# Gated linear attention by levels: multiplying queries and keys in place by exponentials of block totals

## The chip, the cores and the metric

The kernel runs on one core of a Trainium2 chip. A core has a matrix engine (TensorE, PE in the profile, with PEld for the loading of its weights), a vector engine (VectorE, DVE), a scalar engine (ScalarE, ACT), a general engine (GpSimd, POOL) and queues that issue transfers (SyncE, SP, among them). Each engine runs its own list of instructions in order and waits on semaphores for the others. The metric is the device time of one execution in microseconds (us); lower is better.

## The reference, cut to what matters

One decoder layer: a token mixer of two parallel branches, gated linear attention (GLA) and latent attention (MLA), and then a squared-ReLU MLP, each followed by a layer norm. 512 tokens, width 1024, all in float32. The branch that the change touches is GLA, with 4 heads of 128 key channels and 256 value channels:

```python
h = layer_norm(x, ln_in_g, ln_in_b)
q_g, k_g, v_g, r_g, a_lr, q_lat, kv_lat, gate_logits = split(h @ w_in)
log_a = log_sigmoid(a_lr @ w_gla_a2 + b_gla_a2) / 16          # per token and key channel, <= 0
# per head: S_t = diag(exp(log_a_t)) S_{t-1} + k_t^T v_t ;  o_t = q_t S_t, that is
# o_i = sum over j <= i of  ( sum_d q[i,d] k[j,d] exp(b[i,d] - b[j,d]) ) v_j ,   b = running sum of log_a
y_gla = (rms_norm(o) * silu(r_g)) @ w_o_gla
y_mla = softmax attention over q_lat, kv_lat ... @ w_o_mla
g_gla, g_mla = split(sigmoid(gate_logits + b_gate))
out = (g_gla * y_gla + g_mla * y_mla) @ w_out
```

## The kernel before

**Numbers.** Float32 accuracy is had by splitting each operand into a high part and a rest in a narrower format: a product costs three matmuls, high by high, high by rest and rest by high. A helper (`gemm_fm`, L231 to L233 in the profile, and `gemm_tm`, L264 to L266) runs these over 8 slices of the contraction, with four accumulators of 512 columns in PSUM for one section of 512 output columns. Weights come by DMA to `wraw`, ACT writes the high part `whi` (L180), DVE the rest `wlo` (L181).

**Sections and lanes.** The main line is a row of such sections: latents, q, k, then v (value, `proj_v`), r (output gate of GLA, `proj_r`), v, r, then four sections of the branch gates g0 to g3 with the rope part of the MLA queries between them, and so on. After each slice of a section, `tick` advances background generators: `t_lv`, which runs `gla_levels` for heads 0 to 3, and `t_out`, which runs `gla_out`, multiplies the scores by v, normalises and transposes (L735 to L774). A section can only begin in an accumulator when the section before it has been read out of it: for an r section by ACT (`th`, L600) and then DVE (`rg`, L603); for a gate section by ACT (`gt`, L958).

**Levels.** `gla_levels` builds the decayed scores of a head by doubling blocks: s = 1, 2, 4, ... 256. At level s every block of 2s tokens is cut into a left and a right half, and the scores between right queries and left keys need the decay from the key's place to the end of the left half and from the start of the right half to the query. The kernel keeps these exponents in a tile `rp` (row 0 for keys, row 1 for queries, filled by a copy at L623 and a memset at L624). Per level:

- ACT: `E` = exp(rp / 16), 512 columns, with left keys and right queries interleaved (L651);
- DVE: `M` = E times the matching columns of `qk`, written packed; two instructions of 256 columns up to s = 64 (L658), one of 512 above (L654);
- DVE: `advance` adds the block totals into `rp` for the next level (L634);
- PE: two 128x128 matmuls of packed M (L692; s = 128 at L695; for s = 256 transposes at L699);
- DVE: the scores are put into `SD` under a mask (L667), one level later.

For the diagonal, `products` multiplies q by k on POOL (`pr`, L614), ACT copies the high part (L616), POOL subtracts the rest (`qkp`, L617), and PE sums over channels (L682). `products` of the next head is called at level 16.

**What sets the order.** The Python code calls sections and generators in turn; the framework then orders the instructions of each engine by priorities and by its own estimates of durations, and places the waits. Tiles come from pools with a fixed number of buffers.

Of the kernel before, what the change touches and what calls it, by code (L numbers as in the profile page):

```python
# [10 lines left out]
F32 = mybir.dt.float32  # L11
# [8 lines left out]
P = 128  # L20
T = 512
# [31 lines left out]
def tile_hybrid_block(ctx: ExitStack, tc: tile.TileContext, I, out, dbg=None):  # L53
# [234 lines left out]
    for hp in range(2):  # L288
        PL["v", hp] = plan("w_in", C_V + hp * T, T)
        PL["r", hp] = plan("w_in", C_R + hp * T, T)  # L290
    def plan_qr(g):
        PL["qr", g] = plan("w_q_b", NOPE, 4 * ROPE, heads=(HQ, 4 * g, 4), per=4)

    for br in range(2):
        for mb in range(2):
            PL["g", br, mb] = plan("w_in", C_G + br * D + mb * T, T)
        plan_qr(br)

    def plan_pair(pr):
        PL["qn", pr] = plan("w_q_b", 0, 2 * P, heads=(HQ, 2 * pr, 2))  # L300
# [308 lines left out]

    QKP = [None] * GH  # L610

    def products(h, qk):
        pr = B([P, T], F32, "pr")
        gtt(pr, qk[:, 0, :], qk[:, 1, :], op=ALU.mult)  # L614
        QKP[h] = [B([P, T], F32R, "qkp") for _ in range(2)]
        act(QKP[h][0], pr, AF.Copy)  # L616
        gtt(QKP[h][1], pr, f(QKP[h][0]), op=ALU.subtract)  # L617

    def gla_levels(h):
        qk = QK[h]  # L620
        QK[h] = None
        rp = A([P, 2, T], F32, "rp")
        nc.vector.tensor_copy(rp[:, 1, :], GL[h])  # L623
        nc.gpsimd.memset(rp[:, 0, :], 0.0)  # L624
        SD = B([P, NT, P], F32, "SD")
        s128 = kq = None

        def advance(s):
            v = rp[:, 0, :]

            def view(off, side, step):
                return bass.AP(tensor=v.tensor, offset=v.offset + off, ap=[v.ap[0], [side, 2], [2 * s, T // (2 * s)], [step, s]])
            new = view(0, T + s, 1)
            vtt(new, new, view(T + 2 * s - 1, -s, 0), op=ALU.add)  # L634

        def half_lr(t2, s, i):
            v = t2[:, 0, :]
            return bass.AP(tensor=v.tensor, offset=v.offset + 2 * i * P,
                           ap=[v.ap[0], [2 * s, P // s], [T + s, 2], [1, s]])

        def packed(M, s, i):
            v = M[:, i, 0, :]
            return bass.AP(tensor=v.tensor, offset=v.offset,
                           ap=[v.ap[0], [2 * s, P // s], [s + (-2 * P if i else 2 * P), 2], [1, s]])

        def taken(v, s, step):
            return bass.AP(tensor=v.tensor, offset=v.offset + s, ap=[v.ap[0], [step, 2], [2 * s, P // s], [1, s]])

        def vec(s):
            E = B([P, T], F32, "E")  # L650
            act(pairs(E, s), lr(rp, s), AF.Exp, scale=1.0 / 16.0)  # L651
            if s > 64:
                M = B([P, T], F32, "M")
                vtt(pairs(M, s), pairs(E, s), lr(qk, s), op=ALU.mult)  # L654
            else:
                M = B([P, 2, 2, P], F32, "M")
                for i in range(2):
                    vtt(packed(M, s, i), pairs(E[:, 2 * i * P:2 * (i + 1) * P], s), half_lr(qk, s, i), op=ALU.mult)  # L658
# [24 lines left out]
        prev = None  # L683
        while s < T:
            if s == 2:
                vtt(SD, diag.rearrange("p (t i) -> p t i", i=P), ident[:, None, :].to_broadcast([P, NT, P]), op=ALU.mult)
            if s == 16 and h + 1 < GH:
                products(h + 1, QK[h + 1])
            p = PX()
            if s <= 64:  # L690
                for u in range(2):
                    mm(p[:, u * P:(u + 1) * P], M[:, 0, u, :], M[:, 1, u, :], start=True, stop=True)  # L692
            elif s == 128:
                for i in range(2):
                    mm(p[:, i * P:(i + 1) * P], M[:, 2 * i * P:(2 * i + 1) * P],  # L695
                       M[:, (2 * i + 1) * P:(2 * i + 2) * P], start=True, stop=True)
            else:
                for j in range(2):
                    nc.tensor.transpose(p[:, j * P:(j + 1) * P], M[:, j * P:(j + 1) * P], ident)  # L699
                kq = A([P, 2, 2, 256], F32R, "kq")  # L700
                split(M[:, 256:], kq[:, 1, 0], kq[:, 1, 1])
# [11 lines left out]
        act(sd[:, 0, :2], SD[:, :2], AF.Copy)  # L713
        gtt(sd[:, 1, :2], SD[:, :2], f(sd[:, 0, :2]), op=ALU.subtract)
        take(*prev)
        yield
        pt = p[:, :2 * P].rearrange("p (u i) -> p u i", i=P)
        split(pt, sd[:, 0, 2:], sd[:, 1, 2:])
        SS[h] = (sd, s128, kq)
        if h != 2:  # L720
            yield
# [218 lines left out]
            step(t_lv)  # L940

    WID[0] = 3
    proj_v(0)
    proj_r(0)
    finish(t_lat2)
    proj_v(1)
    proj_r(1)
    t_gla = [t_lv, t_out]


    gt = [None] * NK
    for br in range(2):
        for mb in range(2):
            def ev_g(a, ps):
                m = mb * 4 + a
                if gt[m] is None:
                    gt[m] = A([P, 2, T], F32, "gt")
                act(gt[m][:, br, :], ps, AF.Tanh, scale=0.5, bias=hbg[:, br * NK + m:br * NK + m + 1])  # L958
            gemm_fm(PL["g", br, mb], hT, T, ev_g)
        mla_qr(br)  # L960
    hT = None


# [361 lines left out]
```

## Time and profile before

| what | value |
|---|---|
| runs | 887.48, 888.38 and 892.6 us, median 888.38 |
| the profiled execution | 887.85 us |
| its span, first to last instruction | 885.9 us (1.95 us lie outside it) |
| PE busy | 863.7 us |
| DVE busy | 584.4 us |
| ACT busy | 438.9 us |
| POOL busy | 134.1 us |
| the levels on the time axis | first L692 matmul at 104.8 us, last at 253.0 us |

How to read it: "busy" is the time in which an engine had an instruction under way. Idle time of an engine that nobody waits for costs nothing, so what matters is when PE, the busiest, stood still, and what it then waited for. The granted clock (PEclk) is the share of the full TensorE clock; at 0.5 a matmul takes twice as long. In a timeline row the columns are start, duration, engine, line, operation, result<-operands, sizes, count, and in brackets idle time ahead of it and what ended it. Where a row has a count of more than one, its duration is from the first start to the last end.

### The profile page before, as it was taken

How to read it: one execution, taken by the hardware profiler on the slowest of the kernel's cores; microseconds unless marked ns; L12 is line 12 of the kernel's file. 1: busy time of each engine (PE TensorE's matmuls, PEld its weight loads, DVE VectorE, ACT ScalarE, POOL GpSimd, SP SyncE). 2: the span in 40 equal slices, each digit the busy share in tenths (PEclk: the TensorE clock that was granted, in tenths of full speed). 3: DMA queues.
4: the chain of work that ended last, by engine and by line, in shares of the span. 5: the costliest groups of instructions: out<-in, count | busy, mean ns of one | idle time of the engine just before them, and what ended most of it. 6: DMA issues, size and time to landing. Idle time of an engine off the chain costs nothing.

```text
span 885.9 us, 11470 instructions
## 1 busy us (share of the span) xinstructions
PE 863.7 (97%) x4336; PEld 735.9 (83%) x4336; DVE 584.4 (66%) x989; ACT 438.9 (50%) x737; POOL 134.1 (15%) x159
## 2 busy tenths in 40 slices
PE   5999999999999999999999999999999999999995
PEld 5988888887888888888888888988888888888884
DVE  7834894867665234557866797886557646754687
ACT  5546553634444334435654414565457546735661
POOL 2203320111002010000000013004400520242022
PEclk9999999999999999999999999999999999999998
DMA  7413223221323223111307628006941990398075
GB/s 235 145 48 95 72 72 95 72 72 48 90 72 88 74 84 101 54 43 54 116 25 264 190 71 285 1 0 164 293 114 29 260 253 28 71 305 195 1 189 96
DMA packets 63415, 101.13 MB, mean 114 GB/s; under 512 B 7777, under 2 KB 31764, under 8 KB 63360
## 3 DMA queue, kind: packets, MB, share of 16 engines
q1 hardware_dynamic: 48400, 64.04, 23.5%
q0 software_dynamic: 13040, 32.71, 15.5%
q10 hardware_dynamic: 1920, 3.66, 1.2%
q8 instruction: 34, 0.56, 0.3%
q14 instruction: 21, 0.17, 0.1%
HBM read 82.56 MB, written 3.67 MB: 97 GB/s over the span
## 4 chain that ended last, share of the span: by engine, by line
PE 95%; DVE 2%; ACT 1%; DMA 1%; issue 0%; POOL 0%; POOLq 0%; SPq 0%; DVEq 0%; ACTq 0%
PE mm L231 16%; PE mm L232 16%; PE mm L233 16%; PE mm L266 6%; PE mm L264 6%; PE mm L265 6%; PE px L1170 3%; PE px L1172 3%; PE px L1171 3%; PE mm L1170 2%; PE mm L1172 2%; PE mm L1171 2%; PE px L692 1%; PE px L868 1%; PE px L266 1%; PE px L265 1%
## 5 line engine op out<-in xcount | busy, mean ns | idle before, releaser
L181 DVE TENSOR_TENSOR wlo<-wraw,whi 128x1024 fp32r<-128x1024 f32 (+2 forms) x102 | 117.5, 1152 | 137.1 <-ACT whi L180 130.9
L231 PE MATMUL mm<-h,whi 128*128 128x512 f32 x416 | 163.3, 393 | 1.1 <-DVE rg L603 1.1
L232 PE MATMUL mm<-h,whi 128*128 128x512 f32 x416 | 163.0, 392 | 0.0
L233 PE MATMUL mm<-h,wlo 128*128 128x512 f32 x416 | 156.1, 392 | 0.0
L180 ACT ACTIVATE whi<-wraw 128x1024 fp32r<-128x1024 f32 (+2 forms) x102 | 99.9, 979 | 109.6 <-PE mm L232 66.3
L231 PEld LDWEIGHTS mm<-h,whi 128*128 128x128 f32 x416 | 78.6, 189 | 16.9 <-DVE rg L603 1.3
L232 PEld LDWEIGHTS mm<-h,whi 128*128 128x128 f32 x416 | 78.6, 189 | 16.0
L233 PEld LDWEIGHTS mm<-h,wlo 128*128 128x128 f32 x416 | 78.4, 189 | 16.1
L1198 POOL DMA_DIRECT2D res<-ev x54 | 47.5, 985 | 238.0 <-ACT ev L1196 190.7
L265 PE MATMUL mm<-wlo,h 128*128 128x512 f32 x128 | 50.5, 395 | 0.0
L266 PE MATMUL mm<-whi,h 128*128 128x512 f32 x128 | 50.3, 395 | 0.0
L264 PE MATMUL mm<-whi,h 128*128 128x512 f32 x128 | 49.2, 398 | 0.0
L1252 ACT ACTIVATE relu<-mm 128x512 f32<-128x512 f32 x32 | 18.8, 596 | 57.0 <-PE mm L233 57.0
L651 ACT ACTIVATE E<-rp 128x512 f32<-128x512 f32 x36 | 23.9, 665 | 28.3 <-DVE rp L634 27.4
L658 DVE TENSOR_TENSOR M<-E,qk 128x256 f32<-128x256 f32 x56 | 26.7, 501 | 15.4 <-ACT E L651 15.3
L355 POOL TENSOR_TENSOR mv<-mv,mhalf 128x1 f32<-128x1 f32 x4 | 4.1, 1036 | 208.9 <-DVE mv L354 208.9
L180 ACT ACTIVATE xh<-wraw 128x1024 fp32r<-128x1024 f32 (+1 forms) x20 | 19.0, 959 | 26.2 <-PE mm L266 15.0
L181 DVE TENSOR_TENSOR wlo<-wq,whi 128x1024 fp32r<-128x1024 f32 x15 | 18.4, 1224 | 20.3 <-ACT whi L180 20.3
L266 PEld LDWEIGHTS mm<-whi,h 128*128 128x128 f32 x128 | 24.1, 188 | 4.8
L265 PEld LDWEIGHTS mm<-wlo,h 128*128 128x128 f32 x128 | 24.1, 188 | 4.2
L264 PEld LDWEIGHTS mm<-whi,h 128*128 128x128 f32 x128 | 24.0, 188 | 4.1
L1196 ACT ACTIVATE ev<-mm 128x512 f32<-128x512 f32 x20 | 11.9, 600 | 29.6 <-DMA res<-ev 23.7
(400 smaller groups left out, 2223.6 us busy)
## 6 DMA issues: line engine op xcount, KB each, us to landing
wraw<-in_w_in_dram SPq DMA_DIRECT2D x40, 512.0 KB, 3.7
wraw<-in_w_ff_dram SPq DMA_DIRECT2D x32, 512.0 KB, 8.4
wq<-in_w_ff_dram POOLq DMA_DIRECT2D x32, 512.0 KB, 9.8
res<-ev POOLq DMA_DIRECT2D x54, 256.0 KB, 8.7
wraw<-in_w_o_gla_dram SPq DMA_DIRECT2D x8, 512.0 KB, 3.8
wraw<-in_w_o_mla_dram SPq DMA_DIRECT2D x8, 512.0 KB, 3.4
wraw<-in_w_out_dram SPq DMA_DIRECT2D x8, 512.0 KB, 4.3
wraw<-in_w_in_dram SPq DMA_DIRECT2D x8, 360.0 KB, 4.2
```

Of the source, the lines that this page charges most:

```text
L180: st["ins"] = act(hi[:, :nk, :n], raw[:, :nk, :n], AF.Copy)
L181: vtt(lo[:, :nk, :n], raw[:, :nk, :n], f(hi[:, :nk, :n]), op=ALU.subtract)
L231: mm(o, hi[:, c], xh, start=first, stop=False)
L232: mm(o, hi[:, c], xl, start=False, stop=False)
L233: mm(o, lo[:, c], xh, start=False, stop=last)
L264: mm(o, xh, hi[:, :n], start=opens, stop=False, skip_group_check=share)
L265: mm(o, xh, lo[:, :n], start=False, stop=False, skip_group_check=share)
L266: mm(o, xl, hi[:, :n], start=False, stop=last, skip_group_check=share)
L1170: mm(o, xh[:, c], hi[:, pp, cols], start=opens, stop=False, skip_group_check=True)
L1171: mm(o, xh[:, c], lo[:, pp, cols], start=False, stop=False, skip_group_check=True)
L1172: mm(o, xl[:, c], hi[:, pp, cols], start=False, stop=hf == 1 and pp == 1, skip_group_check=True)
L1198: nc.gpsimd.dma_start(res[tt + t][:, j * T:(j + 1) * T], e, accum_op=ALU.add)
```

## The change

The exponents are no longer kept and exponentiated level by level. `totals` (new) builds, on POOL, the sums of log_a over blocks of 2, 4, ... 128 tokens by seven pairwise additions (256, 128, ... 4 columns) into a tile `tot`; ACT takes the exponential of the log decays themselves in place (512 columns) and of all totals (508 columns). Queries are multiplied once by exp of their own decay (DVE). From then on, `grow(s)` multiplies, in place, the queries of right halves and the keys of left halves by the exponential of the total of the other half (DVE, 512 columns, in the place of `advance`). Since `qk` then holds what the level needs, packing is a copy: two ACT copies of 256 columns for each level up to 64 (`pack`); levels 128 and 256 read `qk` directly. `rp`, its copy and its memset, `E`, and the multiplications into `M` are gone. `totals` of the next head is called where `products` is, at level 16. A second edit changes the order of the gate sections: g0, g2, rope, g1, g3, rope in the place of g0, g1, rope, g2, g3, rope; the weight plan and the calls both follow one table.

```diff
+    ORDER = (("v", 0), ("r", 0), ("v", 1), ("r", 1), ("g", 0), ("g", 2), ("qr", 0), ("g", 1), ("g", 3), ("qr", 1))
...
+    def totals(h):
+        t = TOT[h] = B([P, T], F32, "tot")
+        src, o, n = GL[h], 0, T // 2
+        while n >= 4:
+            a = src.rearrange("p (n two) -> p n two", two=2)
+            src = t[:, o:o + n]
+            gtt(src, a[:, :, 0], a[:, :, 1], op=ALU.add)
+            o += n
+            n //= 2
+        act(GL[h], GL[h], AF.Exp, scale=1.0 / 16.0)
+        act(t[:, :o], t[:, :o], AF.Exp, scale=1.0 / 16.0)
...
     def gla_levels(h):
         qk = QK[h]
         QK[h] = None
-        rp = A([P, 2, T], F32, "rp")
-        nc.vector.tensor_copy(rp[:, 1, :], GL[h])
-        nc.gpsimd.memset(rp[:, 0, :], 0.0)
         SD = B([P, NT, P], F32, "SD")
...
-        def advance(s):
...
-            new = view(0, T + s, 1)
-            vtt(new, new, view(T + 2 * s - 1, -s, 0), op=ALU.add)
+        def grow(s):
+            new = view(qk[:, 0, :], 0, T + s, 2 * s, 1, s)
+            tot, o = (GL[h], 0) if s == 1 else (TOT[h], T - 2 * T // s)
+            vtt(new, new, view(tot, o + 1, -1, 2, 0, s), op=ALU.mult)
...
-        def vec(s):
-            E = B([P, T], F32, "E")
-            act(pairs(E, s), lr(rp, s), AF.Exp, scale=1.0 / 16.0)
-            if s > 64:
-                M = B([P, T], F32, "M")
-                vtt(pairs(M, s), pairs(E, s), lr(qk, s), op=ALU.mult)
-            else:
-                M = B([P, 2, 2, P], F32, "M")
-                for i in range(2):
-                    vtt(packed(M, s, i), pairs(E[:, 2 * i * P:2 * (i + 1) * P], s), half_lr(qk, s, i), op=ALU.mult)
-            if s < 256:
-                advance(s)
+        def pack(s):
+            M = B([P, 2, 2, P], F32, "M")
+            for i in range(2):
+                act(packed(M, s, i), half_lr(qk, s, i), AF.Copy)
             return M
...
         if h == 0:
+            totals(0)
             products(0, qk)
+        vtt(qk[:, 1, :], qk[:, 1, :], GL[h], op=ALU.mult)
         s = 1
-        M = vec(1)
+        M = pack(1)
...
             if s == 16 and h + 1 < GH:
+                totals(h + 1)
                 products(h + 1, QK[h + 1])
...
+            if s < 256:
+                grow(s)
             s *= 2
-            if s < T:
-                M = vec(s)
+            if s <= 64:
+                M = pack(s)
             yield
```

What this does to the instruction lists shows best at the end of the second r section, where head 2 is in its upper levels and the first gate section is about to begin. After the change the lines have other numbers: the level matmuls are L702 (s = 128: L705), the output transposes L786, `th` L604, `rg` L607, `gss` L772 and `grs` L774, the packs L667, the two exponentials L627 and L628, `grow` L649, the first multiplication of the queries L685, the additions L624, `pr`, its copy and `qkp` L632, L634 and L635.

On PE, the last rows of that r section and the first of the gate section, before (M of levels 32 and 64, then the gate section in the accumulator `mm_2008`):

```order
L264 MATMUL mm_1749<-whi_1869,h_33_171 128x512
L265 MATMUL mm_1749<-wlo_1870,h_33_171 128x512
L266 MATMUL mm_1749<-whi_1869,h_33_171 128x512
L692 MATMUL px_1954<-M_1924 128x128 x2
L692 MATMUL px_1999<-M_1960 128x128 x2
L231 MATMUL mm_2008<-h_12_115,whi_1938 128x512
```

and now:

```order
L265 MATMUL mm_1731<-wlo_1841,h_33_171 128x512
L702 MATMUL px_1931<-M_1902 128x128 x2
L266 MATMUL mm_1731<-whi_1840,h_33_171 128x512
L702 MATMUL px_1974<-M_1936 128x128 x2
L705 MATMUL px_1995<-qk_750 128x128 x2
L231 MATMUL mm_1979<-h_12_115,whi_1915 128x512
```

The two matmuls of level 128 moved ahead of the gate section; before, they stood 36 section matmuls later.

On ACT at the same place, before (E of levels 32 and 64 among the two output transposes `ogT`, then `th`):

```order
L616 ACTIVATE qkp_1914<-pr_1912 128x512
L651 ACTIVATE E_1922<-rp_1753 128x512
L109 ACTIVATE ogT_1928<-px_1895,cb 128x512
L651 ACTIVATE E_1958<-rp_1753 128x512
L109 ACTIVATE ogT_1964<-px_1931,cb 128x512
L600 ACTIVATE th_1979<-mm_1737 128x512
```

and now:

```order
L180 ACTIVATE whi_1915<-wraw_1838 128x1024
L627 ACTIVATE g_666<-g_666 128x512
L634 ACTIVATE qkp_1893<-pr_1891 128x512
L667 ACTIVATE M_1902<-qk_750 128x4x2x32 x2
L109 ACTIVATE ogT_1905<-px_1864,cb 128x512
L667 ACTIVATE M_1936<-qk_750 128x2x2x64 x2
L109 ACTIVATE ogT_1939<-px_1908,cb 128x512
L628 ACTIVATE tot_1881<-tot_1881 128x508
L604 ACTIVATE th_1954<-mm_1719 128x512
```

Each E became two packs, and the two exponentials of head 3 (L627, L628) stand ahead of `th`.

On POOL, the same stretch before (`grs` is the inverse root for head 1, `rp` the memset for head 3):

```order
L762 TENSOR_TENSOR grs_1837<-gss_1722,mhalf 128x4
L614 TENSOR_TENSOR pr_1912<-qk_752 128x512
L617 TENSOR_TENSOR qkp_1915<-pr_1912,qkp_1914 128x512
L624 MEMSET rp_2093 128x512
L714 TENSOR_TENSOR sd_2071<-SD_1756,sd_2071 128x256
```

and now:

```order
L774 TENSOR_TENSOR grs_1810<-gss_1704,mhalf 128x4
L624 TENSOR_TENSOR tot_1881<-g_666 128x256
L632 TENSOR_TENSOR pr_1891<-qk_752 128x512
L624 TENSOR_TENSOR tot_1881<-tot_1881 128x128
L624 TENSOR_TENSOR tot_1881<-tot_1881 128x64
L635 TENSOR_TENSOR qkp_1894<-pr_1891,qkp_1893 128x512
L624 TENSOR_TENSOR tot_1881<-tot_1881 128x32
L624 TENSOR_TENSOR tot_1881<-tot_1881 128x16
L624 TENSOR_TENSOR tot_1881<-tot_1881 128x8
L624 TENSOR_TENSOR tot_1881<-tot_1881 128x4
L726 TENSOR_TENSOR sd_2039<-SD_1735,sd_2039 128x256
```

The seven additions stand around `pr` and `qkp`, four of them behind `qkp`.

More of the change, by code (lines that the diff above doesn't have):

```diff
@@ L287, in tile_hybrid_block @@
     PL["k"] = plan("w_in", C_K, T)
-    for hp in range(2):
-        PL["v", hp] = plan("w_in", C_V + hp * T, T)
-        PL["r", hp] = plan("w_in", C_R + hp * T, T)
+    ORDER = (("v", 0), ("r", 0), ("v", 1), ("r", 1), ("g", 0), ("g", 2), ("qr", 0), ("g", 1), ("g", 3), ("qr", 1))
     def plan_qr(g):
         PL["qr", g] = plan("w_q_b", NOPE, 4 * ROPE, heads=(HQ, 4 * g, 4), per=4)
[L294 to L297, printed above, removed]
+    for sec, i in ORDER:
+        if sec == "v":
+            PL["v", i] = plan("w_in", C_V + i * T, T)
+        elif sec == "r":
+            PL["r", i] = plan("w_in", C_R + i * T, T)
+        elif sec == "g":
+            PL["g", i // 2, i % 2] = plan("w_in", C_G + i * T, T)
+        else:
+            plan_qr(i)
     def plan_pair(pr):
@@ L610, in tile_hybrid_block @@
     QKP = [None] * GH
+    TOT = [None] * GH
+    def totals(h):
[9 more added lines that the diff above has]
+        act(t[:, :o], t[:, :o], AF.Exp, scale=1.0 / 16.0)
     def products(h, qk):
@@ L942, in tile_hybrid_block, with gates, ev_g @@
     WID[0] = 3
[L943 to L947, printed above, removed]
     t_gla = [t_lv, t_out]
     gt = [None] * NK
[L952 to L960, printed above, removed]
+    def gates(br, mb):
+        def ev_g(a, ps):
+            m = mb * 4 + a
+            if gt[m] is None:
+                gt[m] = A([P, 2, T], F32, "gt")
+            act(gt[m][:, br, :], ps, AF.Tanh, scale=0.5, bias=hbg[:, br * NK + m:br * NK + m + 1])
+        gemm_fm(PL["g", br, mb], hT, T, ev_g)
+    for sec, i in ORDER:
+        if sec == "v":
+            proj_v(i)
+        elif sec == "r":
+            proj_r(i)
+            if i == 0:
+                finish(t_lat2)
+        elif sec == "g":
+            gates(i // 2, i % 2)
+        else:
+            mla_qr(i)
     hT = None
```

13 lines of the change are left out of this document (6 added, 7 removed).

## The prediction

> **What bounds the kernel now.** I read the page's busy times and its chain first, then PE's busy time by stretches, then the timeline of the place where PE stood still.
>
> ```profile
> PE 863.7 (97%) x4336; PEld 735.9 (83%) x4336; DVE 584.4 (66%) x989; ACT 438.9 (50%) x737; POOL 134.1 (15%) x159
> PE 95%; DVE 2%; ACT 1%; DMA 1%; issue 0%; POOL 0%; POOLq 0%; SPq 0%; DVEq 0%; ACTq 0%
> ...
> 0.00:50.00 50.00, 39.81 (x236) 38.52 (x237) 35.93 (x86) 25.20 (x43) 11.57 (x21) 1.00 0.54 168
> 175.00:200.00 25.00, 25.00 (x132) 21.42 (x131) 17.85 (x34) 10.93 (x23) 4.16 (x3) 1.00 0.23 64
> 200.00:225.00 25.00, 23.37 (x114) 19.38 (x113) 18.23 (x31) 10.56 (x19) 1.86 (x3) 0.93 0.23 65
> 250.00:275.00 25.00, 24.71 (x145) 21.46 (x145) 11.75 (x23) 11.88 (x26) 4.89 (x6) 1.00 0.22 64
> 800.00:886.00 86.00, 76.15 (x348) 63.35 (x346) 59.06 (x81) 42.40 (x60) 13.93 (x16) 0.97 0.50 117
> ```
>
> In the stretch rows stand length, then busy time of PE, PEld, DVE, ACT and POOL, then the granted clock. The span is a row of matmuls. Of the 885.9 - 863.7 = 22.2 us in which PE stood still, 50 - 39.81 = 10.2 lie in the first 50 us and 86 - 76.15 = 9.9 in the last 86, where the change does nothing. Between, where the levels run, PE loses 1.63 us in 200 to 225 and 0.29 in 250 to 275. So an engine beside PE that gets lighter gives nothing by itself; only waits of PE count. The stretch at 200 has also the one clock below 1.00. Its rows:
>
> ```profile
> 195.14 0.60 PE L692 MATMUL px<-M 128*128 128x128 f32 x4
> 195.50 0.48 PE L266 MATMUL mm<-whi,h 128*128 128x512 f32 x1
> ...
> 203.99 0.39 PE L266 MATMUL mm<-whi,h 128*128 128x512 f32 x1
> 204.22 0.60 PE L692 MATMUL px<-M 128*128 128x128 f32 x4
> 205.37 0.68 PE L692 MATMUL px<-M 128*128 128x128 f32 x4 [0.55 <-DVE M L658]
> 207.13 0.50 PE L231 MATMUL mm<-h,whi 128*128 128x512 f32 x1 [1.08 <-DVE rg L603]
> ...
> 208.17 0.60 PE L232 MATMUL mm<-h,whi 128*128 128x512 f32 x1
> ...
> 211.55 0.42 PE L232 MATMUL mm<-h,whi 128*128 128x512 f32 x1
> ```
>
> A section matmul takes 0.23 us from start to start (203.99 to 204.22), a level's pair 0.36 (195.14 to 195.50). Without waits the two pairs from 204.22 would end at 204.22 + 2 x 0.36 = 204.94; the gate section began at 207.13. That is **2.19 us** of waiting, first for M, then for `rg`, which empties the accumulator. Then the eight steps from 208.17 to 211.55 take 3.38 us instead of 8 x 0.227 = 1.82: another **1.56 us** at half clock. Together 3.75 us, nearly all that can be won here.
>
> A rule of the Trainium skill bears on the second number: TensorE: Matmul & The Clock Gate, section Why this matters for your kernels, asks for no idle gap above about 3 us, since one idle window takes the clock back. By that rule gaps of 0.55 and 1.08 us would cost no clock, and only 2.19 us could be won. The rows speak against it; I go by them.
>
> **The change part by part.**
>
> ```profile
> L658 DVE TENSOR_TENSOR M<-E,qk 128x256 f32<-128x256 f32 x56 | 26.7, 501 | 15.4 <-ACT E L651 15.3
> L651 ACT ACTIVATE E<-rp 128x512 f32<-128x512 f32 x36 | 23.9, 665 | 28.3 <-DVE rp L634 27.4 <-DVE rp L623 0.9
> L634 DVE TENSOR_TENSOR rp<-rp 128x512 f32<-128x512 f32 x32 | 23.1, 722 | 0.0
> L654 DVE TENSOR_TENSOR M<-E,qk 128x512 f32<-128x512 f32 x8 | 5.5, 685 | 0.7 <-ACT E L651 0.7
> L651 ACT ACTIVATE E<-rp x36: 616/634/878, 98.4 to 251.7; 128x512 f32<-128x512 f32 x36
> 212.97 0.42 ACT L106 ACTIVATE kq<-M 128x256 fp32r<-128x256 f32 x1 [0.76 <-DVE M L654]
> 172.74 0.75 POOL L714 TENSOR_TENSOR sd<-SD,sd 128x256 fp32r<-128x256 f32 x1 [8.32 <-ACT sd L713]
> 103.22 0.51 POOL L453 TENSOR_TENSOR kr<-kt,kt 128x64 f32<-128x64 f32 x1
> 212.85 0.42 DVE L623 COPY rp<-g 128x512 f32<-128x512 f32 x1
> ```
>
> - DVE loses 26.7 (56 L658) + 5.5 (8 L654) + 4 x 0.42 (L623) = 33.9 us. `grow` takes the place of L634 with the same 32 instructions over the same columns, so I carry 23.1 over. Four query multiplications of 512 columns like L654 add 4 x 0.69 = 2.7. Net -31 us, none of it on PE's path as such.
> - ACT loses 23.9 and gains eight exponentials at the median 0.63 (5.1) and 56 packs. No row shows ACT writing runs as short as one number; the nearest copy of 256 columns takes 0.42, and the slowest E against its median, 878 / 634, bounds the short runs at 0.58; twice the copy, 0.84, is my far end, and the 0.39 of an `osq` of 256 columns (row further down) the near one. I take 0.42, the nearest row: 23.5. Net +4.7 us, +3 at the near end and +28 at the far one; ACT is busy 10.9 of 25 us in the stretch at 175, so its idle time holds either, except where PE waits in line behind it.
> - POOL gains 28 additions and loses four memsets, which I leave out. 256 columns: 0.75. The six smaller ones lie between nothing and that; the nearest row, 64 columns, has 0.51. At 0.51 a head costs 0.75 + 6 x 0.51 = 3.8, at 0.75 throughout 5.25: +15 us, at most +21, on an engine that is idle 85% of the time.
> - PE keeps its matmuls and transposes, with other operands. SP's transfers keep their order. The gate sections g1 and g2 change places: same shapes, same readers (`gt` on ACT), and the tiles of `gt` 4 to 7 are taken a section later; no PE wait hangs on them, so nothing.
> - A level's loop was E 0.63, first M, `advance` 0.68; it becomes two packs 0.84 and `grow` 0.68: the same 1.5 to 1.7 us.
>
> **The place that decides** is the end of the second r section. ACT there has head 3's two exponentials ahead of `th`, and the second of them waits for POOL's seventh addition, which stands behind `qkp`, which waits for ACT's copy of `pr`. `th`, `rg` and so the gate section wait behind all this.
>
> ```profile
> 190.09 0.39 ACT L757 ACTIVATE osq<-px 128x256 f32<-128x256 f32 x1 [4.13 <-PE px L755]
> 190.99 1.05 ACT L180 ACTIVATE whi<-wraw 128x1024 fp32r<-128x1024 f32 x1
> 203.65 0.67 ACT L109 ACTIVATE ogT<-px,cb 128x512 fp32r<-128x512 f32 x1
> 204.22 1.56 ACT L600 ACTIVATE th<-mm 128x512 f32<-128x512 f32 x3
> ...
> 190.85 1.02 POOL L762 TENSOR_TENSOR grs<-gss,mhalf 128x4 f32<-128x4 f32 x1 [16.91 <-DVE gss L760]
> 191.83 1.60 POOL L614 TENSOR_TENSOR pr<-qk 128x512 f32<-128x512 f32 x1
> 198.41 2.25 POOL L617 TENSOR_TENSOR qkp<-pr,qkp 128x512 fp32r<-128x512 f32 x1 [4.98 <-ACT qkp L616]
> ...
> 192.18 1.53 DVE L658 TENSOR_TENSOR M<-E,qk 128x256 f32<-128x256 f32 x1
> 193.63 1.21 DVE L181 TENSOR_TENSOR wlo<-wraw,whi 128x1024 fp32r<-128x1024 f32 x1
> 206.40 0.68 DVE L603 SCALAR_TENSOR_TENSOR rg<-th,mm 128x512 f32<-128x512 f32 x1
> ...
> L767 DVE SCALAR_TENSOR_TENSOR og<-px,grs,rg 128x256 f32<-128x256 f32 x16 | 6.6, 473 | 0.0
> ```
>
> PE would be ready for the gate section at 204.94 + 0.36 = 205.3, since level 128 now stands ahead of it. `osq` at 190.09 waits for PE, so both orders start there. I walk the new one from its end, 190.5, with these durations (packs 0.42, `grow` and `rg` 0.68, an exponential 0.63, `th` 1.56 / 3 = 0.52, the copy of `pr` 0.6), in two ways.
>
> *DVE unhindered by POOL.* Level 4's packs with the weight copy between them end at 192.4, DVE's `wlo` at 193.15, `grow` 193.85, four `og` 195.75, `grow` 196.4, packs of 16 at 197.25, then weight copy, head 3's exponential and the copy of `pr` 199.55, packs of 32 at 200.4, `ogT`, packs of 64 at 201.95, the second `ogT` 202.6. POOL's `qkp` ends at 201.8, four additions at 203.85, the totals' exponential at 204.5, `th` 205.0, `rg` **205.7**. PE waits 0.4 us instead of losing 3.75: 887.85 - 3.35 = 884.5.
>
> *DVE held by POOL.* The row at 192.18 shows an M of 256 columns at 1.53 us, where the mean of its group is 0.50; it began inside `pr` (191.83 to 193.43) and ended 0.28 after it. If each DVE multiplication or subtraction that meets POOL fares so: first addition 192.6, `wlo` behind it 193.8, `pr` 195.4, `grow` 196.1, `og` 198.0, `grow` 198.7, packs of 16 at 199.55, the copy of `pr` 201.8, `qkp` 204.05, `grow` behind it 204.7, packs of 64 at 205.55, the second `ogT` 206.2, the last four additions at 0.75 each 207.05, exponential 207.7, `th` 208.2, `rg` **208.9**. PE waits 3.6 us and then loses the 1.56 of the clock: 5.15 instead of 3.75, so 889.25.
>
> The Trainium skill has the rule behind this, SBUF — State Buffer, section Who interferes with whom: a DVE instruction with two SBUF inputs is blocked by a GpSimd instruction that reads SBUF, for its whole length, and whichever starts first wins. It speaks against this change, which adds 28 such instructions. The row agrees (1.53 against 0.50); L181 at 193.63, begun after `pr`, has its normal 1.21. By the rule in full the sum is 889.25, without it 884.5.
>
> I take the middle, since who starts first decides, and half of the meetings may go either way: `rg` near 207.3, a wait of 2.0 us, hardly less than the 2.19 of now. If the clock drops again, PE loses 3.55, a gain of 0.2; if it doesn't, a gain of 1.75. Between them 1.0: 887.85 - 1.0 = 886.9. The median of the runs lies 0.5 above the profiled execution, so I forecast 886.9 + 0.5 = **887.4 us**.
>
> Elsewhere the trace has no PE wait on a level (25.00 of 25.00 at 175), but the new order puts pairs closer. The tightest I see is head 0's second pair.
>
> ```profile
> 105.05 0.60 PE L692 MATMUL px<-M 128*128 128x128 f32 x4
> 92.54 2.73 DVE L476 COPY qk<-mm 128x512 f32<-128x512 f32 x4 [1.31 <-PE mm L233]
> 96.66 1.40 DVE L110 SCALAR_TENSOR_TENSOR latT<-px,cb,latT 128x512 fp32r<-128x512 f32 x2
> 100.37 0.21 DVE L450 TENSOR_TENSOR kt<-lat,cs 128x64 f32<-128x64 f32 x1
> 103.76 0.72 ACT L557 ACTIVATE krh<-kr 128x256 fp32r<-128x256 f32 x2 [1.62 <-POOL kr L453]
> ```
>
> The first pair now stands 12 section matmuls earlier, at 105.05 - 12 x 0.227 = 102.3, the second 20 later, at 102.3 + 0.36 + 4.54 = 107.2. Its packs need, on DVE, the query multiplication after 92.54 + 2.73 = 95.3, then a `wlo`, twelve `kt` of 0.21 at most, two `latT` and `grow`: 95.3 + 0.69 + 1.21 + 2.52 + 1.40 + 0.68 = 101.8; on ACT then two packs, both `krh` and a weight copy: 101.8 + 0.84 + 0.72 + 1.05 = 104.4. That leaves 2.8 us, which holds packs of 0.84 too.
>
> **The rivals.** (1) The wait all but goes, as in the first walk: 884.5 + 0.5 = 885.0. For it: ten M of 0.50 us, 5 us of DVE work, stood ahead of `rg` and go. Against it: `th` gets POOL's chain in its way. (2) Slower than before: additions, exponential of totals, `th`, `rg`, as in the second walk: 889.25 + 0.5 = 889.8; with the ten packs between `osq` and `th` at 0.58 instead of 0.42 another 1.6, 891.4. It decides once `rg` ends after 205.3 + 2.19 = 207.5. (3) Packs at 0.84: 10 x 0.42 = 4.2 more there, and 1 us at each of the three other heads: 889.8 + 4.2 + 3 = 897. (4) Nothing that PE sees changes, since `rg` waits as long as now: 888.4, which lies in the forecast's range.
>
> **How the numbers follow.** The forecast, `rg` between 206.3 and 208 with or without the clock drop, and rival 4: 0.50, own range 885.7 to 888.8. Rival 1: 0.18. Rival 2: 0.25. Rival 3: 0.06. Something unseen: 0.01. The range from 884.6 to 890.6 takes in rival 1 and most of rival 2. One per cent, 8.9 us, is about what a measurement of this kernel can tell from no change. No more than 3.75 can be won, so faster by over 1% gets 0.01; slower by over 1% needs 897.3, part of rival 3: 0.04; within 1%: 0.95.
>
> **What would show it.** Right: DVE about 31 us less busy, ACT some 5 more, POOL some 15 more; the first matmul of the gate section between 205.7 and 208.9, its wait named after `rg`, and `th` behind an ACT wait for `tot`; a clock below 1.00 there only behind such a wait. Wrong: packs well above 0.42 us; PE waits named after M or `qk` in other stretches; ACT waiting for `tot` ahead of `vh`; many `grow` rows at 1.3 us or more, which would make rival 2 the rule.

## The result and the profile after

The changed kernel takes **883.67 us** (median of 6 runs, 882.95 to 884.43), the kernel before beside it 888.32 us (6 runs, 886.78 to 892.6). The ratio is 0.9944, with a 95% interval of 0.9922 to 0.9965: 4.65 us or 0.56% faster. The forecast was 887.4 with a range down to 884.6, so the time lies 0.9 us below the range; "within 1%" came true. The profiled execution took 884.43 us, its span 882.7, against 887.85 and 885.9. In all that follows, two disturbed runs (1458 and 1244 us, at granted clocks of 0.56 and 0.66) are left out.

The busy row of the changed kernel's page, and its two stretches in which PE lost time before (length, then busy time of PE, PEld, DVE, ACT and POOL, then the granted clock):

```profile
PE 861.4 (98%) x4336; PEld 734.1 (83%) x4336; DVE 565.1 (64%) x925; ACT 442.2 (50%) x765; POOL 138.9 (16%) x183
...
200.00:225.00 25.00, 24.66 (x133) 20.98 (x132) 17.23 (x27) 12.45 (x26) 3.61 (x6) 1.00 0.29 85
250.00:275.00 25.00, 25.00 (x145) 22.00 (x144) 9.57 (x22) 9.74 (x23) 4.41 (x5) 1.00 0.29 85
```

PE stood still for 1.63 us in the first of them and 0.29 in the second; now it is 0.34 and nothing, and the clock is full in both. The end of the second r section in PE's timeline, with the level of 128 now ahead of the gate section:

```profile
204.89 0.60 PE L702 MATMUL px<-M 128*128 128x128 f32 x4
205.25 0.48 PE L266 MATMUL mm<-whi,h 128*128 128x512 f32 x1
205.57 0.60 PE L702 MATMUL px<-M 128*128 128x128 f32 x4
206.01 0.61 PE L705 MATMUL px<-qk 128*128 128x128 f32 x4
206.96 0.50 PE L231 MATMUL mm<-h,whi 128*128 128x512 f32 x1 [0.34 <-DVE rg L607]
207.29 0.40 PE L232 MATMUL mm<-h,whi 128*128 128x512 f32 x1
...
208.45 0.40 PE L231 MATMUL mm<-h,whi 128*128 128x512 f32 x1
```

The wait for M is gone, the one for `rg` is 0.34 us instead of 1.08, and the five steps behind 207.29 take 0.23 each: no half clock.

**A measure that does not scatter.** The fifteen profiles reach the k section, ahead of all levels, at 70.9 to 72.2 us, so I compare times between two marks on PE: the start of its 289th section matmul (in the k section) and of its 1537th (in the MLA branch, behind the levels). Section matmuls are those of `gemm_fm` and `gemm_tm`, L231 to L233 and L264 to L266. The marks in the timelines of before and of after:

```profile
71.22 0.39 PE L231 MATMUL mm<-h,whi 128*128 128x512 f32 x1
...
405.14 0.39 PE L231 MATMUL mm<-latT,whi 128*128 128x512 f32 x1
```

```profile
72.19 0.39 PE L231 MATMUL mm<-h,whi 128*128 128x512 f32 x1
...
401.90 0.39 PE L231 MATMUL mm<-latT,whi 128*128 128x512 f32 x1
```

Before 333.92 us, after 329.71: 4.21 us less. Behind the second mark the two profiles keep the same distance to the end of PE's work. Worked out in the same way for the experiments:

| kernel | between the marks, us |
|---|---|
| before; once more (c2); with late loads (m1) | 333.92; 332.59; 332.61 |
| new gate order alone (e2) | 331.66 |
| new levels alone (e1) | 330.51 |
| the change; again (c1); again (c3) | 329.71; 329.70; 329.74 |
| packs on DVE (e4); twice (e9) | 329.81; 337.74 |
| `th` copied once (e5); three times (e6) | 330.18; 331.16 |
| additions on DVE (e3b); twice on POOL (e8); on DVE, late loads (m2) | 329.50; 329.45; 329.50 |

Like kernels agree within 0.04 us, except the first profile of before, which has 1.33 more. From the second mark to the end of PE's work all profiles take 471.0 us, except e2 (477.2) and m1 and m2 (470.7); of these below.

### The profile page after: what moved, and what is told of

It is laid out like the page before. It is cut to its first block, busy times and chain, and to the rows that moved or that the text cites. A ratio compares the mean times of both kernels' runs of the same rounds, so it can differ in the third digit from the quotient of the medians.

```text
span 882.7 us, 11469 instructions
## 1 busy us (share of the span) xinstructions
PE 861.4 (98%) x4336; PEld 734.1 (83%) x4336; DVE 565.1 (64%) x925; ACT 442.2 (50%) x765; POOL 138.9 (16%) x183
## 4 chain that ended last, share of the span: by engine, by line
PE 96%; DMA 2%; DVE 1%; issue 0%; ACT 0%; POOLq 0%; DVEq 0%; SPq 0%; POOL 0%; ACTq 0%
PE mm L231 16%; PE mm L232 16%; PE mm L233 16%; PE mm L266 6%; PE mm L265 6%; PE mm L264 6%; PE px L1186 3%; PE px L1188 3%; PE px L1187 3%; PE mm L1187 2%; PE mm L1188 2%; PE mm L1186 2%; PE px L702 1%; PE px L880 1%; PE px L264 1%; PE px L266 1%
## 5 line engine op out<-in xcount | busy, mean ns | idle before, releaser
L231 PE MATMUL mm<-h,whi 128*128 128x512 f32 x416 | 162.5, 392 | 0.3 <-DVE rg L607 0.3
L233 PE MATMUL mm<-h,wlo 128*128 128x512 f32 x416 | 155.6, 391 | 0.0
L231 PEld LDWEIGHTS mm<-h,whi 128*128 128x128 f32 x416 | 78.1, 188 | 16.4 <-DVE rg L607 0.5
L233 PEld LDWEIGHTS mm<-h,wlo 128*128 128x128 f32 x416 | 77.9, 188 | 15.9
L266 PE MATMUL mm<-whi,h 128*128 128x512 f32 x128 | 50.5, 394 | 0.0
L264 PE MATMUL mm<-whi,h 128*128 128x512 f32 x128 | 48.8, 395 | 0.0
L667 ACT ACTIVATE M<-qk 128x256 f32<-128x256 f32 x56 | 23.9, 455 | 16.5 <-DVE qk L649 16.2
L649 DVE TENSOR_TENSOR qk<-qk,tot 128x512 f32<-128x512 f32 x28 | 21.6, 770 | 10.2 <-ACT M L667 7.2
L266 PEld LDWEIGHTS mm<-whi,h 128*128 128x128 f32 x128 | 24.1, 188 | 4.8
L264 PEld LDWEIGHTS mm<-whi,h 128*128 128x128 f32 x128 | 24.0, 188 | 4.4
L1129 POOL DMA_DIRECT2D wq<-in_w_ff_dram x32 | 24.0, 922 | 11.3 <-PE mm L265 5.9
```

Of the source, the lines that this page charges most:

```text
L231: mm(o, hi[:, c], xh, start=first, stop=False)
L233: mm(o, lo[:, c], xh, start=False, stop=last)
L264: mm(o, xh, hi[:, :n], start=opens, stop=False, skip_group_check=share)
L266: mm(o, xl, hi[:, :n], start=False, stop=last, skip_group_check=share)
```

## The experiments

Every kernel was timed beside the kernel before, and ratios are to it.

**Which of the two edits (e1, e2).** e1 is the change with the old gate order, e2 the kernel before with the new one:

```diff
-    ORDER = (..., ("g", 0), ("g", 2), ("qr", 0), ("g", 1), ("g", 3), ("qr", 1))
+    ORDER = (..., ("g", 0), ("g", 1), ("qr", 0), ("g", 2), ("g", 3), ("qr", 1))
```

> The changed kernel with the gate sections back in the old order (g0, g1, rope, g2, g3, rope); everything else as changed. Theory A (all of the gain comes from the levels: 3.1 us at the end of the second r section, 1.1 us at the end of the second gate section): 883.7 us, ratio to before 0.995, first gate matmul after a wait of about 0.3 us and no wait of PE for gt near 262 us. Rival B (the wait for gt went because the gate sections changed places): a wait of PE for gt of about 0.3 us is back near 262 us and 0.7 to 1.1 us of the gain are lost, 884.4 to 884.8. Rival C (the order carries most): above 886.

> The kernel before with the new order of the gate sections alone. Theory A: 888.3 us, ratio 1.000, PE waits for M (0.5) and rg (1.1) at the end of the second r section and half clock behind them, PE's wait for gt near 266 us still there. Rival B: the wait for gt is gone, 887.2 to 887.6. Rival C: 885 or less.

Measured: e1 884.87 us, ratio 0.996 (0.9945 to 0.9976); e2 887.53, ratio 1.000 (0.9978 to 1.0023), its runs in two groups, up to 888.1 and from 891.8 (the lower and the upper kind, of which below). Between the marks e1 is 2.08 us shorter than c2 and m1, e2 0.93, both together 2.88. By the marks theory A falls: the gate order does bring its part, by rival B's price of 0.7 to 1.1 us; the ratio of e2 alone doesn't show it. The place is the end of the second gate section, where PE waits for `gst` and then for `gt`. PE and then ACT in c2 (kernel before):

```profile
262.77 0.38 PE L753 MATMUL px<-gst,kq 128*128 128x256 f32 x1
263.14 0.39 PE L753 MATMUL px<-vh,sd 128*128 128x256 f32 x1
...
263.98 0.39 PE L754 MATMUL px<-gst,kq 128*128 128x256 f32 x1
264.20 0.28 PE L755 MATMUL px<-gst,kq 128*128 128x256 f32 x1
264.78 0.39 PE L264 MATMUL mm<-whi,latT 128*128 128x256 f32 x1 [0.29 <-ACT gt L958]
...
262.62 0.38 ACT L757 ACTIVATE osq<-px 128x256 f32<-128x256 f32 x1
262.88 0.20 ACT L757 ACTIVATION_READ_ACCUMULATOR osq<-px 128x1 f32 x1
264.04 0.69 ACT L958 ACTIVATE gt<-mm,hbg 128x512 f32<-128x512 f32 x1 [0.95 <-PE px L754]
```

A step from start to start is 0.12 us there; five of them, at 262.77, 263.14, 263.98, 264.20 and 264.78, take 0.22 to 0.58 instead, **1.00 us** more in all, of which the profile lists 0.29 as a wait.

The same end in the changed kernel:

```profile
261.64 0.28 PE L767 MATMUL px<-vh,sd 128*128 128x256 f32 x1
261.76 0.29 PE L264 MATMUL mm<-whi,latT 128*128 128x256 f32 x1
...
258.48 2.05 ACT L963 ACTIVATE gt<-mm,hbg 128x512 f32<-128x512 f32 x3 [2.33 <-PE mm L233]
```

With the old order head 3's matmuls on `gst` stand on PE, and the first `osq` on ACT, ahead of the section change; ACT waits 0.95 us for PE, and PE then for ACT. With the new order `gt` of three tiles is done first and the rope section follows without a stop. e1, with the old order, has the stop again, named after `gst`, and loses 0.95 us over its usual steps there:

```profile
262.72 0.39 PE L766 MATMUL px<-gst,kq 128*128 128x256 f32 x1 [0.24 <-DVE gst L107]
```

The sections have equal shapes; what differs is how the framework lays head 3's output among them. That is read from the rows; no run moved head 3's output alone.

**Again (c1, c3).** The changed kernel, unaltered.

> The changed kernel once more, timed beside the other kernels of this group. Theory A2 (formed from the last group: growth brings the 3.1 us at the end of the second r section, the order of the gate sections the 1.1 us at the end of the second gate section): 1.0 us below growth alone by ratio, 0.9945 to 0.9955 of before, again no wait of PE for gt or gst near 262 us. Rival G (growth alone does all, the two kernels differ by scatter): 0.996 of before.

> The changed kernel once more, as the measure for the next. Theory M (the upper kind comes from the meeting of SP's third load of the first MLP weight with POOL's loads of the second, near 530 us; the change only shifts the odds): lower kind at 883 to 884.5, and a run near 889 may occur, since one of the relatives of this kernel (additions made twice) had three of nine there. Rival S (the change removed the upper kind for good): none above 886.

Measured: c1 883.85 us, ratio 0.9923 (0.9896 to 0.995); c3 884.24, ratio 0.9959 (0.9945 to 0.9973), no wait for `gt` or `gst`. The ratio moves with the kernel before: beside c1 its median was 892.17, since 13 of its 24 runs were of the upper kind, and beside c3 887.29. By ratio c3 cannot be told from e1 (0.996); the marks tell them apart, 329.70 to 329.74 against 330.51, and rival G falls by them. c3 has no run near 889, which both of its theories allow.

**Where the half clock comes from (c2, e5, e6).** c2 is the kernel before. e5 and e6 hold the changed kernel's `rg` back:

```diff
             act(th, ps, AF.Tanh, scale=0.5)
+            if hp == 1 and a == 0:
+                for _ in range(1):    # e6: 3
+                    act(th, th, AF.Copy)
```

> The kernel before once more, for its profile alone. Theory N (the half clock behind the waits for M and rg comes in some executions only, as in the kernel with the new gate order, where the same waits of 0.55 and 1.08 us were followed by full clock): the same two waits, and either clock. Theory H (these waits always bring it): clock near 0.55 for 3 us behind them. Either way a wait for gt of 0.3 us near 266.

> The changed kernel with one extra in-place copy on ACT of th of the first tile of the second r section, which holds rg back; in the instruction order it falls behind the next two th, so that rg comes about 2 x 0.52 + 0.6 + 0.2 = 1.9 us later and PE waits about 2.2 us in one piece at the place that decided the prediction. Theory W (a wait costs its length and no more): 885.6 us. Theory H (behind a wait of about 1.6 us or more the clock falls to half and costs 1.56 us besides): 887.1. Theory N (the fall comes in some executions and not in others, since the kernel with the new gate order alone had the same two waits, 0.55 and 1.08, at full clock): runs spread between the two, and the profile shows either.

> As the last one, with three such copies, which fall behind further ACT work: rg about 5.2 us later, one wait of PE of about 5.5 us. Theory W: 888.9 us. Theory H: 890.5, granted clock below 0.8 in the 4 us behind the wait in the profile. Theory N: between, either in the profile.

c2 took 886.5 us, with the same two waits and no half clock behind them:

```profile
205.66 0.68 PE L692 MATMUL px<-M 128*128 128x128 f32 x4 [0.54 <-DVE M L658]
207.43 0.50 PE L231 MATMUL mm<-h,whi 128*128 128x512 f32 x1 [1.08 <-DVE rg L603]
207.77 0.40 PE L232 MATMUL mm<-h,whi 128*128 128x512 f32 x1
...
209.83 0.39 PE L233 MATMUL mm<-h,wlo 128*128 128x512 f32 x1
```

Nine steps in 2.06 us, 0.23 each. e2 and m1 have the same waits and full clock too: **of four profiles with these waits one had the half clock**, at a price of 1.56 us by its eight slow steps. (The whole way differs by 1.33 only, since c2, m1 and e2 lose 0.31 us near 109 us, where the first profile does not.) Theory N holds, H falls. e5 (884.51 us) and e6 (885.88) missed their sizes: the instruction order took `rg` of the second tile first, so the waits were 0.82 us, in e6 0.82 and 0.40, not 2.2 and 5.5. What e5 shows is that a wait without half clock costs its length once PE stops anyway: its wait is 0.48 longer than the change's, and its way 0.47. A second stop costs more: in e6 the listed waits are 0.88 longer, and the way 1.45.

**DVE ahead of rg (e4, e9).** The packs on DVE, once and twice:

```diff
-                act(packed(M, s, i), half_lr(qk, s, i), AF.Copy)
+                nc.vector.tensor_copy(packed(M, s, i), half_lr(qk, s, i))    # e9: in a loop of two
```

> The changed kernel with the 56 packing copies on DVE instead of ACT. Theory A (it was DVE's load ahead of rg that made PE wait in the kernel before): ten copies of 0.25 to 0.5 us stand ahead of rg again, rg 1 to 3.5 us later, PE waits 1.3 to 3.8 us there and the clock falls to half behind it if the waits reach about 1.6 us: 884.7 to 888.7 us. Rival F (th and rg hang on POOL's additions and the exponential of the totals, not on DVE's load): 883.7, the wait for rg stays at 0.3 us, since ACT gets 24 us lighter and the chain over POOL is unchanged.

> The packs on DVE as in the run before, and each copy made twice there (0.30 us a copy, ten copies between osq and rg, so 3.0 us more DVE work ahead of rg; nothing else changes). Theory D (the load of DVE ahead of rg and of M is what made PE wait in the kernel before; with packs on DVE once it stood 0.4 us from the edge): waits for M and rg of 2 to 3.5 us together are back at the end of the second r section, 886 to 889 us. Rival F (the chain over POOL and ACT sets it, DVE has room): at most 0.5 us more than with the packs on DVE once, 884.7 or less.

e4: 884.22 us, ratio 0.9948 (0.9926 to 0.9969). Its packs took 0.29 us (median), the lower half of what was expected, PE waited 0.36 for M and not for `rg`: giving the packs to ACT brings nothing that can be measured. e9: 892.67 us, ratio 1.0021 (1.0001 to 1.0042) beside the same runs of the kernel before as c1, more than expected. PE in e9, and the stretch behind the wait:

```profile
206.53 0.68 PE L703 MATMUL px<-M 128*128 128x128 f32 x4 [0.55 <-DVE M L668]
210.39 1.19 PE L703 MATMUL px<-M 128*128 128x128 f32 x4 [3.18 <-DVE M L668]
211.24 0.78 PE L231 MATMUL mm<-h,whi 128*128 128x512 f32 x1
...
212.00:214.00 2.00, 2.00 (x7) 1.55 (x6) 2.00 (x5) 0.00 (x0) 0.00 (x0) 0.60 0.28 109
...
PE mm L231 <- DVE rt L456: 1.6, 1, 1.6
```

Rival F falls, and theory D holds in kind: with DVE loaded again PE waits for M, 0.55 + 3.18 us, the clock falls behind the long wait, and further waits of 1.6 us (for `rt`, at 281 us) and 0.7 us (for `vl`) open elsewhere. The size is not the copies' alone. Between the doubled packs of the late level the framework set a weight rest (`wlo`, 1.21 us at 208.30), and the doubled copies lengthen the making of M itself, so e9 does not tell DVE's load from that.

**POOL's additions and DVE (e3, e3b, e8).** The additions moved to DVE, and doubled on POOL:

```diff
-            gtt(src, a[:, :, 0], a[:, :, 1], op=ALU.add)
+            vtt(src, a[:, :, 0], a[:, :, 1], op=ALU.add)    # e3, e3b; e8: gtt, made twice
```

> The changed kernel with the 28 additions of totals on DVE instead of POOL. They no longer hold DVE from POOL; pr and qkp still can. Theory A (after the change DVE's load and its collisions with POOL no longer decide; only 0.3 us of wait are left there): 883.2 to 884.0 us, rg of the second r section within 0.7 us of where it was, DVE busy about 7 to 10 us more for 28 additions. Rival D (POOL's additions still cost PE something by holding DVE): 882.7 or less. Rival E (DVE has no room for 1.7 us a head more): rg later by 1 us or more, 884.7 or more.

> The additions of totals on DVE once more, for a profile, since the last one was taken at a clock of 0.56. Theory A2: no multiplication of grow above 1 us except beside pr and qkp, rg of the second r section within 0.7 us of the change's, PE's wait there between 0 and 0.5 us; 28 additions on DVE of 0.1 to 0.4 us, 6 to 8 us in all.

> The changed kernel with each addition of totals made twice on POOL (28 more, some 10 us), so that DVE meets POOL twice as often; the exponential of the totals then falls behind the first th in the instruction order. Theory A2 (DVE has 0.5 us to spare at the deciding place, holds of 1.1 us each): more grow rows above 1.2 us than the 4 or so of the change, PE waits at the end of the second r section up to 1 us: 883.7 to 884.9 us, 0.995 to 0.996 of before. Rival D (the collisions are what is left of the cost): 885.5 or more. Rival F (nothing): 883.7.

e3: 883.74 us, ratio 0.9942 (0.9922 to 0.9963); e3b, for the profile: 882.88. e8: 884.05, ratio 0.9962 (0.9937 to 0.9987), three of its nine runs at 888.7 to 889.9, the others at 883.0 to 884.5. `grow` behind level 1 in the change, then in e3b (duration in ns, least, median and most):

```profile
L649 DVE TENSOR_TENSOR qk<-qk,tot x28: 676/692/1775, 106.8 to 249.2; 128x512 f32<-128x512 f32 x28
```

```profile
L649 DVE TENSOR_TENSOR qk<-qk,tot x28: 676/692/721, 105.1 to 247.7; 128x512 f32<-128x512 f32 x28
```

The holds are real: in the change five DVE multiplications are above 1 us (three `grow`, two of the queries); in e3b no `grow` is, and one of the queries still is. But PE's way is only 0.21 us shorter in e3b, and 0.26 in e8 with twice the additions. Neither has a wait for `rg`. What they share is that the first `th` stands ahead of the totals' exponential in the instruction order; the holds went in one and stayed in the other. So that order is the likely cause, though no run changes it alone. Rival D falls.

**The upper kind of run (m1, m2).** In e2's profile, which is of the upper kind, PE lost 6.1 us against before near 541 us, far behind the change; 4.13 of it stand in one row, and the granted clock is 0.50 for 3.4 us from 544.8 on. ACT's wait for a load of the first MLP weight, and PE's stop behind it. (It is the sixth load of that weight in the trace; the expectations call it the third.)

```profile
541.56 1.06 ACT L180 ACTIVATE whi<-wraw 128x1024 fp32r<-128x1024 f32 x1 [6.30 <-DMA wraw<-in_w_ff_dram]
...
543.58 0.44 PE L374 MATMUL px<-ca,res 128*128 128x128 f32 x2 [4.13 <-ACT lnt L379]
```

In before's first profile the same copy waited 1.27 us. There SP's sixth load was issued ahead of POOL's first load of the second MLP weight (SP's row holds the fifth load and the sixth, the sixth from 532.13):

```profile
531.00 1.50 SPq L168 DMA_DIRECT2D wraw<-in_w_ff_dram  x2
...
532.80 1.53 POOL L1113 DMA_DIRECT2D wq<-in_w_ff_dram  x2 [3.82 <-PE mm L265]
```

In e2 it stood at 530.80, behind POOL's 530.74. Both m1 (from the kernel before) and m2 (from e3) move POOL's loads:

```diff
-        if ci == 0:
-            win_load(0)
...
                 t_r1 = spawn(residual1())
+                win_load(0)
```

> The kernel before, with one step moved far behind the changed stage: the first eight loads of the second MLP weight on POOL's queue are issued after the first section of the first MLP matrix instead of ahead of it. Seen so far: runs of the kernel before lie at 886 to 889.5 or at 892 to 894.5, runs with the new levels at 883 to 886 alone; and in the one profile of the upper kind PE waits 6.1 us near 541 us, since the third load of the first MLP weight on SP's queue was issued 0.06 us behind POOL's first (10.7 us to land), where it stood 0.67 us ahead of it in the profile of before (5.7 us) and 1.19 us in that of the change (5.0 us). Theory M (this meeting of two queues makes the upper kind): no run above 890, median 886 to 888.5. Rival S (the upper kind has another cause): runs at 892 and above as often as in the kernel before beside it.

> The changed kernel with the additions of totals on DVE (no wait of PE for rg in its profile) and POOL's eight loads of the second MLP weight issued after the first section, so that they meet nothing. Theory M: no run above 886, median 0.3 to 0.8 us below the changed kernel, 883.0 to 883.5. Rival S: runs near 889 here as there. Rival V (late loads make the sums of the second weight late): 885 or more.

m1: 886.65 us, ratio 0.998 (0.9962 to 0.9997), none of 12 runs above 888.82, while 5 of 23 of the kernel before beside it were above 889.5. m2: **883.37 us** (882.78 to 883.68), ratio 0.9948 (0.9936 to 0.9961), against 884.24 for c3 beside it; rival V falls. This fits theory M. It doesn't prove it: with odds of 5 in 23, twelve runs without one come by luck one time in twenty, and only one profile of the upper kind was taken. Late loads also help a little without the stop: behind the second mark m1 and m2 are 0.35 us shorter than their like.

Of the kernel before, 25 of 90 runs in all were above 889.5; of the changed kernel none of 17; of e8, which has the new levels, three of nine. So the new levels can have the stop. Counting runs more than 3.4 us above the fastest of their kernel, it came in 29 of 102 with the old levels (before and e2) and in 3 of 81 with the new ones (the change, e1, e3 to e6, e8, e9): rarer in these runs. That fits the issue times. SP's sixth load was 0.67 and 0.51 us ahead of POOL's first and 0.06 behind it in the three profiles with old levels, and 0.74 to 1.19 us ahead in ten with new ones. No run tests whether the lead is the cause.

## Why the prediction failed, point by point

**The bound was too low: "nearly all that can be won", 3.75.** That sum held for the one place. *The gate order* stood outside it at nothing, "no PE wait hangs on them, so nothing": it is worth 0.93 us (e2 against c2), the stops at `gst` and `gt`. The 0.29 us of the last of them stood in my own first fence, in the stretch at 250, and I did not follow it to its row; the stops there cost 1.00 us, more than three times what the stretch row shows, because the matmuls' modelled ends cover the rest. *A second stop* is not in the first profile, on which I built, but in c2, m1 and e2: near 109 us PE starts a pair of head 0 late and loses 0.31 us. In c2 an M of 256 columns at 103.62 took 1.51 us beside POOL's `pr` (103.11 to 104.85), and the M of that pair came at 108.91 instead of 108.31. No profile with the new levels shows a stop there.

**The middle between the walks was the wrong pick.** `rg` began at 206.22 in a profile that runs 0.97 us late by the first mark, so it was done by about 205.9; the first walk had 205.7, the second 208.9, my middle 207.3. The wait of 2.0 us that I forecast was 0.34. (A pair ahead of another pair takes 0.44 us, 205.57 to 206.01 in the change, not 0.36; so the old stops were 2.11 us and not 2.19, and PE was ready 0.16 later than I had it.) The rows of the changed kernel:

```profile
194.31 1.77 DVE L649 TENSOR_TENSOR qk<-qk,tot 128x512 f32<-128x512 f32 x1
196.01 1.65 DVE L779 SCALAR_TENSOR_TENSOR og<-px,grs,rg 128x256 f32<-128x256 f32 x4
201.13 1.77 DVE L685 TENSOR_TENSOR qk<-qk,g 128x512 f32<-128x512 f32 x1
...
201.08 1.28 POOL L635 TENSOR_TENSOR qkp<-pr,qkp 128x512 fp32r<-128x512 f32 x1 [4.37 <-ACT qkp L634]
202.32 1.87 POOL L624 TENSOR_TENSOR tot<-tot 128x32 f32<-128x32 f32 x4
...
203.88 0.73 ACT L667 ACTIVATE M<-qk 128x256 f32<-128x256 f32 x2 [1.69 <-DVE qk L649]
204.51 0.67 ACT L109 ACTIVATE ogT<-px,cb 128x512 fp32r<-128x512 f32 x1
205.08 0.61 ACT L628 ACTIVATE tot<-tot 128x508 f32<-128x508 f32 x1
205.60 1.56 ACT L604 ACTIVATE th<-mm 128x512 f32<-128x512 f32 x3
```

The holds came as half expected: less the 0.97, `og` ended at 196.7, between 195.75 and 198.0, and the packs of 64 at 203.6, in the middle of 201.95 and 205.55. What did not follow is that `rg` moves with them. In the first walk `th` waits for POOL's additions, which end at 203.85, while ACT has the second `ogT` done at 202.6; so the first 1.25 us of a delay on DVE's chain are free. That chain brought the second `ogT` to 204.2, 1.6 us late. POOL's chain was not late at all: its last four additions took 1.87 us, not 4 x 0.75, and ended at 204.19 - 0.97 = 203.2. So the totals' exponential waited for `ogT` on its own engine, not for POOL, and `rg` came only about 0.2 us behind the first walk. Two half risks on two chains that run side by side do not add up to a middle.

**The half clock was priced as if it always came.** I put 1.56 us into the gain of the first walk as certain. Three of four profiles with the old waits do without it. (Nor was the stretch at 200 the only one below full clock, as I wrote: the row of 800 to 886 has 0.97, but the change does nothing there.) The Trainium skill's rule (TensorE: Matmul & The Clock Gate, Why this matters for your kernels: no idle gap above about 3 us) fares better than I gave it: e9's wait of 3.18 us and e2's of 4.13 brought the fall, 0.82 and 1.08 mostly did not; but the fall behind 0.55 + 1.08 in the first profile is no case of it, and why it came there stays open.

**What stood.** PE bounds, and only its waits counted: 31 us less work for DVE (the groups of the pages give 57.0 us removed and 29.2 added, so 27.8; the page's busy time fell by 19.3) gave 2.08 us. Packs took 0.42 us:

```profile
L667 ACT ACTIVATE M<-qk x56: 399/416/716, 97.9 to 238.8; 128x256 f32<-128x256 f32 x56
L624 POOL TENSOR_TENSOR tot<-tot x24: 202/294/848, 77.8 to 204.0; 128x128 f32<-128x128 f32 x4, 128x64 f32<-128x64 f32 x4, 128x32 f32<-128x32 f32 x4, 128x16 f32<-128x16 f32 x4
L624 POOL TENSOR_TENSOR tot<-g x4: 605/621/1122, 77.2 to 192.7; 128x256 f32<-128x256 f32 x4
```

ACT grew by 3.3 us against 4.7. POOL's additions were priced at 0.51 and 0.75 and have medians of 0.29 and 0.62, 12.3 us in all against 15; the page's POOL time grew by 4.8 alone, since the memsets went and other POOL rows got shorter. The Trainium skill's rule on the SBUF port (SBUF — State Buffer, Who interferes with whom) is borne out by 1.77 us against 0.69, and by e3b, where `grow` stays below 0.73 without the additions. As a price on PE it was 0.2 us or less in the changed kernel. Of the rivals the first described the place, at 885.0; the slower one and packs at 0.84 did not come. "One per cent" as what a measurement can tell was too coarse: the interval of the ratio is 0.9922 to 0.9965.

**The sum.** Summed step by step, from start to start and over the usual step of each shape, the change wins 2.88 us against c2: 1.53 at the end of the second r section (the old stops cost 2.11, the new one 0.58), 1.00 at the end of the second gate section, 0.31 near 109 us and 0.04 spread over the rest. Against the first profile it is 4.21: 1.53, 1.00, the half clock's 1.57 and 0.1 spread over the rest. The rest of 4.65 is how the runs fell: beside c3, with one upper run in nine, the medians differ by 3.05.

## What to carry to other kernels

Follow every stop of the bounding engine to its row, also the 0.3 us ones, before calling a number all that can be won: equal sections in another order can shift a neighbour's work across a section change. When runs scatter by as much as the effect, compare the time between two marks of the bounding engine's own stream; here it repeats within 0.04 us and splits a gain of 2.9 us into its parts. A load taken off a side engine pays only up to the edge at which the bounding engine stops waiting for it, and e4 and e9 show how near that edge can lie: 0.36 us of waiting with one copy, 3.7 with two and the order that came with them.

## What was unexpected of the hardware

- The same two waits of 0.55 and 1.08 us were followed by half clock for 3.4 us in one execution and by full clock in three. Waits of 3.18 us (e9) and 4.13 us (e2) were each followed by half clock for 3.4 us.
- A transfer's time went with 0.7 us of order: the sixth load of the first MLP weight landed after 5.7 us when it was issued 0.67 us ahead of POOL's first load, and after 10.7 us when 0.06 us behind it, and PE's work there took 6.1 us longer, half clock included.
- A step in a row of starts can mislead: a 512-column section matmul behind 128-column ones takes 0.31 us to the next start instead of 0.23, with no wait shown, but the last 128-column one ahead of it takes 0.03 instead of 0.11. The two cancel: with every step at the usual length of its kind, before and the change take 328.57 and 328.55 us between the marks, though the change has five such places fewer.
